# One hybrid decoder block on one Trainium2 core: the issue order of every engine drawn up on another machine model

## The chip, the core and the metric

The kernel runs on one core of a Trainium2 chip. The metric is the device time of one execution in microseconds (us); a median of several runs is given. TensorE (PE) does the matmuls, VectorE (DVE), ScalarE (ACT) and GpSimd (POOL) the elementwise work, and SyncE (SP) issues nearly all the DMA transfers. Each engine works through its own list of instructions in order; an instruction that must wait for another engine or for a transfer holds up everything behind it in its list.

## The reference, cut to what matters

Sequence 1024, width 1024, everything in float32, one layer:

```python
u = rms_norm(x, norm_mix)
u_ssm, q, k, v, f_logit, gate_logits = split(u @ w_in)
y_ssm = gelu(s5_ssm(u_ssm, ...))                     # 32 groups of 16 channels, 64 complex states
glu_a, glu_b = split(y_ssm @ w_glu);  out_a = glu_a * sigmoid(glu_b)
out_b = forgetting_attention(q, k, v, f_logit) @ w_fox_o      # 8 heads of 64, causal
...                                                  # the two branches are merged by sigmoid gates
h = x + merged @ w_mix_out
h = h + memory_cross_attention(rms_norm(h), rms_norm(mem), ...)  # 4 heads of 128, 256 memory tokens
h = h + swiglu_ffn(rms_norm(h))                      # hidden width 2816
out = rms_norm(h, norm_final)
```

## The kernel before, in words

**Arithmetic.** Every float32 operand of a matmul is split into a high part (a cast to fp32r on ACT, `split`, L178) and a low part (a subtraction on DVE or POOL, L179). A product is three matmuls: high by high, high by low, low by high (`mm3`, L168 to L170).

**Weights.** `wload` (L148 to L158) loads a block of up to 512 KB into a buffer `raw` (two buffers, DMA at L153; `stage_in` has its own at L384) and splits it into `whi` and `wlo` (four buffers each). A load can be issued only when the split of the block two loads earlier has run.

**Stages, in the order of the text.**

- `stage_in`: norms and transposes of `mem` and `x` (tiles `xt`, loaded at L351), keys and values of the memory (`w_mem_kv`), the first part of `w_in`. The small parameters of the state-space branch (`prow`, `ldr`, `craw`, `b_re`, `b_im`, `dbc`, L1132 to L1148) are loaded here too.
- `stage_ssm`: the state-space branch, with the gate logits' GEMM beside it.
- `Fox`: the attention, head by head: projections of later heads (weights loaded at L1540 and L1541), row maxima (`row_max`, L1593, and `max_row`, which sends them through the DMA `hb<-mr`, L1610), scores (L1620 to L1633), values (L1645 to L1654), and the division. During the last heads the outputs `yh`, `yl` of the state-space branch (L1698) and blocks of `wg_d` (gating weights, L153) are loaded for what follows.
- `stage_tail`: outputs of the two branches (`Glu`, `fox_part`), the mix, the memory attention (`mem_out` is its output projection), the FFN and the last norm.

**FFN.** The products go by a seven-product scheme for 2x2 blocks (`prod`, L868; the seven activation blocks are A11, A12, S4, A22, S1, S2, S3). The loop runs over 22 blocks j of the hidden width. `start(j)` does A11 and A12, `middle(j)` S2, S3 and S1, `end(j)` S4 and A22. L896 reads the bank after S4, L898 and L899 after A22, and L900 on POOL makes `g`. `w_first`, `w_sums` and `w_last` prepare the weights from `raw` and `rawb` (`w_fetch`, L805); `w_last` splits the last pair, `wdh` and `wdl`, and is the last reader of `raw`. `gated` stores sums of `g` (`c_d`), and `out_fetch` and `out_sums` prepare the second GEMM's weights (`t_d`). The second GEMM (`o_mm`, L1005) comes after the loop. PSUM has eight banks: mm 3, sc 2, pv 2, misc 1.

**What sets the order.** The text interleaves the stages by hand: an order string in `stage_in`, `weave` and `filler` lists elsewhere, and some edges "issue this after that" (`issue_after`). Within these and the data dependences, the tile framework's scheduler decides when the block `with TileContext` closes. It runs through a model of the machine and picks, for each engine, which ready instruction comes next. The semaphore waits follow from the list that results. The framework has two such models.

## Time and profile before

| what | value |
|---|---|
| median of 3 runs | 1588.8 us (1587.95 to 1590.42) |
| span of the profiled execution, first to last instruction | 1586.7 us |
| PE busy in the span | 1534.0 us, 97% |
| DVE, ACT, POOL busy | 1019.5, 655.2, 254.3 us |
| mean granted TensorE clock | 0.988 |

For the profiled execution only its span is given; the median of the other executions lies 2.1 us above it. In the profile a row reads: start, duration, engine, line, operation, destination<-sources. SPq rows are the issues of transfers, not the transfers.

### The profile page before, as it was taken

Reading aid. Unit: us, or ns where it says so; the run is one execution under the profiler, and the core shown is the slowest. Engines: PE = TensorE matmul, PEld = TensorE weight load, DVE = VectorE, ACT = ScalarE, POOL = GpSimd, SP = SyncE. Lnnn points to the kernel's source line nnn. Section 1 sums busy time; section 2 is a strip of 40 time slices with the busy share of each in tenths; the row PEclk is TensorE's granted clock in tenths of the full one; section 3 lists DMA queues with packets and bytes.
Section 4 is the critical chain, followed back from the end, with each engine's and each line's share of the span. In section 5 each row is a group of like instructions: output and inputs, shape, how many; then the busy total and the mean of one; then the engine's idle time right before and its main releaser. Section 6 shows DMA issues by size and latency. Waiting matters only on the chain.

```text
span 1586.7 us, 20446 instructions
## 1 busy us (share of the span) xinstructions
PE 1534.0 (97%) x7313; PEld 1261.3 (79%) x7313; DVE 1019.5 (64%) x1850; ACT 655.2 (41%) x1173; POOL 254.3 (16%) x335
## 2 busy tenths in 40 slices
PE   7799999999999899999999999999999999999997
PEld 6578888898777668888888778888888888788885
DVE  6666445344688687675555697766677776565555
ACT  6422434323576553222435564333333333254342
POOL 2027653200212124110002200100000000000001
PEclk8899999999999999999999999999999999999999
DMA  7764445652023736357412186555444554796642
GB/s 266 125 132 80 127 131 110 130 145 30 18 52 48 186 95 208 125 172 259 160 46 75 54 283 239 170 164 163 155 153 160 166 162 156 261 391 223 195 150 106
DMA packets 197940, 240.86 MB, mean 152 GB/s; under 512 B 35448, under 2 KB 126488, under 8 KB 197328
## 3 DMA queue, kind: packets, MB, share of 16 engines
q1 hardware_dynamic: 191216, 223.84, 48.2%
q10 hardware_dynamic: 6624, 15.73, 2.6%
q8 instruction: 57, 0.93, 0.2%
q14 instruction: 43, 0.35, 0.1%
HBM read 165.60 MB, written 75.86 MB: 152 GB/s over the span
## 4 chain that ended last, share of the span: by engine, by line
PE 75%; DVE 8%; DMA 7%; issue 4%; POOL 3%; ACT 2%; SPq 1%; DVEq 0%; POOLq 0%; ACTq 0%
PE mm L868 14%; PE mm L168 7%; PE pv L868 7%; PE mm L170 7%; PE mm L169 7%; PE mm L1005 4%; PE sc L868 3%; PE sc L1005 3%; PE pv L1005 3%; PE sc L168 3%; PE sc L169 3%; PE sc L170 3%; DMA raw<-in_w_in_dram 2%; PE misc L1005 1%; PE pv L168 1%
## 5 line engine op out<-in xcount | busy, mean ns | idle before, releaser
L179 DVE TENSOR_TENSOR wlo<-raw,whi 128x1024 fp32r<-128x1024 f32 (+2 forms) x121 | 132.0, 1094 | 135.1 <-ACT whi L178 133.9
L178 ACT CAST whi<-raw 128x1024 fp32r<-128x1024 f32 (+2 forms) x124 | 116.1, 940 | 220.0 <-DMA raw<-in_w_ffn_in_dram 54.1
L168 PE MATMUL mm<-uh,whi 128*128 128x512 f32 x344 | 138.8, 404 | 2.8 <-ACT whi L178 2.7
L170 PE MATMUL mm<-uh,wlo 128*128 128x512 f32 x344 | 136.5, 397 | 1.7 <-DVE wlo L179 1.7
L169 PE MATMUL mm<-ul,whi 128*128 128x512 f32 x344 | 136.4, 396 | 0.0
L179 DVE TENSOR_TENSOR ol<-or,oh 128x1024 fp32r<-128x1024 f32 x73 | 89.3, 1224 | 71.6 <-ACT oh L178 70.3
L178 ACT CAST oh<-or 128x1024 fp32r<-128x1024 f32 x73 | 76.8, 1052 | 105.3 <-PE mm L1005 33.6
L900 POOL TENSOR_TENSOR g<-a,c 128x512 f32<-128x512 f32 x22 | 35.2, 1600 | 392.8 <-ACT a L899 373.9
L170 PEld LDWEIGHTS mm<-uh,wlo 128*128 128x128 f32 x344 | 65.7, 191 | 16.5 <-DVE wlo L179 3.1
L1630 POOL TENSOR_TENSOR pl<-pf,ph 128x512 fp32r<-128x512 f32 (+1 forms) x32 | 39.7, 1239 | 241.1 <-DVE ph L1629 196.1
L168 PEld LDWEIGHTS mm<-uh,whi 128*128 128x128 f32 x344 | 65.9, 192 | 15.5 <-ACT whi L178 3.2
L169 PEld LDWEIGHTS mm<-ul,whi 128*128 128x128 f32 x344 | 66.0, 192 | 11.3
L197 POOL TENSOR_TENSOR r<-ms,mhalf 128x1 f32<-128x1 f32 x26 | 15.1, 582 | 354.9 <-DVE ms L193 344.5
L1627 ACT ACTIVATE pf<-sc 128x512 f32<-128x512 f32 (+1 forms) x96 | 46.5, 490 | 46.3 <-DVE sc L1623 28.6
L868 PE MATMUL pv<-S3h,we 128*128 128x512 f32 x176 | 58.1, 389 | 0.0
L1633 DVE TENSOR_TENSOR pl<-pf,ph 128x512 fp32r<-128x512 f32 (+2 forms) x64 | 35.1, 550 | 10.2 <-ACT ph L1632 9.5
L1005 PE MATMUL mm<-oh 128*128 128x512 f32 x106 | 41.2, 389 | 0.0
L1005 PE MATMUL mm<-ol,oh 128*128 128x512 f32 x106 | 41.2, 389 | 0.0
L1005 PE MATMUL mm<-oh,ol 128*128 128x512 f32 x106 | 41.2, 389 | 0.0
L168 PE MATMUL mm<-yh,whi 128*128 128x512 f32 x104 | 40.9, 393 | 0.0
L168 PE MATMUL sc<-uh,whi 128*128 128x512 f32 x104 | 40.8, 393 | 0.0
L170 PE MATMUL mm<-yh,wlo 128*128 128x512 f32 x104 | 40.6, 390 | 0.0
(580 smaller groups left out, 4537.5 us busy)
## 6 DMA issues: line engine op xcount, KB each, us to landing
or<-c_d SPq DMA_DIRECT2D x77, 256.0 KB
raw<-in_w_in_dram SPq DMA_DIRECT2D x22, 512.0 KB
wo<-in_w_ffn_out_dram SPq DMA_DIRECT2D x22, 512.0 KB
c_d<-g SPq DMA_DIRECT2D x44, 256.0 KB
t_d<-wo SPq DMA_DIRECT2D x44, 256.0 KB
or<-t_d SPq DMA_DIRECT2D x44, 256.0 KB
raw<-in_w_ffn_in_dram SPq DMA_DIRECT2D x20, 512.0 KB
rawb<-in_w_ffn_in_dram SPq DMA_DIRECT2D x20, 512.0 KB
```

The source lines that it names most:

```text
L168: T.matmul(ps, lh, rh, start=first, stop=False)
L169: T.matmul(ps, lh, rl, start=False, stop=False)
L170: T.matmul(ps, ll, rh, start=False, stop=last)
L178: self.A.copy(hi, src)
L179: (self.G if pool_lo else self.V).tensor_sub(lo, src, f32(hi))
L197: self.G.tensor_tensor(out=r, in0=v, in1=self.mhalf[:, 0:n], op=ALU.pow)
L868: T.matmul(ps, l_[:, k, :], r_, start=first and k == 0 and i == 0, stop=k == 3 and i == 2, skip_group_check=True)
L900: G.tensor_mul(g[:, 512:], a1, c1)
L1005: T.matmul(ps, l_[:, gi], r_[:, 512:], start=n < 3 and p == 0 and k == 0 or n == 7 and p == 0 and k == 0, stop=p == NP - 1 and k == 2, ski ...
L1627: self.exp = A.activation(pf[:, off:], ps[:, off:], AF.Exp)
L1630: G.tensor_sub(pl[:, off:], pf[:, off:], f32(ph[:, off:]))
L1633: V.tensor_sub(pl[:, off:], pf[:, off:], f32(ph[:, off:]))
```

## The change

The scheduler is told to run on its timeline model instead of its core model. It is one argument; no instruction of the kernel's text is changed, added or removed.

```diff
-    with _tile.TileContext(nc) as tc:
+    with _tile.TileContext(nc, schedule_with_timeline_sim=True) as tc:
         hybrid_block_kernel(tc, *args)
```

Laid side by side, the two issue orders have the same counts on every engine. On PE an instruction moves by 18 places in the mean, by up to 120 at most; on DVE by 4 in the mean, on ACT and SP by 2, on POOL by less than one. The places of the larger moves are `stage_in` (small parameters earlier in SP's list), the last heads of `Fox`, `mem_out` with the entry to the FFN, and the FFN loop. From the second FFN GEMM to the end the lists are the same.

For the FFN loop the order on PE is, each name being a product of 12 matmuls:

```text
before: A11(j) A12(j) S4(j-1) A22(j-1) S2(j) S3(j) S1(j) | A11(j+1) ...
after:  S4(j) S2(j+1)x2 A22(j) S2(j+1)x10 S3(j+2) A11(j+3)x2 A12(j+3)x2 S1(j+1) A11(j+3)x10 A12(j+3)x10 S4(j+1) ...
```

(the second line shows a part of a pattern that spans two blocks).

## The prediction

> **What bounds the kernel now.** I read the page first (busy times, slices, chain), then the table by stage, then single rows at the places where the issue order changes.
>
> ```profile
> span 1586.7 us, 20446 instructions
> PE 1534.0 (97%) x7313; PEld 1261.3 (79%) x7313; DVE 1019.5 (64%) x1850; ACT 655.2 (41%) x1173; POOL 254.3 (16%) x335
> PEclk8899999999999999999999999999999999999999
> PE 75%; DVE 8%; DMA 7%; issue 4%; POOL 3%; ACT 2%; SPq 1%; DVEq 0%; POOLq 0%; ACTq 0%
> raw<-in_w_ffn_in_dram SPq DMA_DIRECT2D x20, 512.0 KB
> ```
>
> PE is busy for 97% of the span, and three quarters of the chain that ends last is PE. The change alters no instruction, only the order in which each engine issues them. An order cannot shorten 1534.0 us of matmuls; it can only remove or add idle time of PE. What there is to remove is 1586.7 − 1534.0 = 52.7 us, and the table by stage says where (stretch, length, PE busy, PEld, DVE, ACT, POOL, granted clock, DMA share, GB/s):
>
> ```profile
> 0.00:80.00 80.00, 61.42 (x307) 50.17 (x307) 54.13 (x140) 43.40 (x74) 13.85 (x16) 0.85 0.75 194
> 80.00:500.00 420.00, 413.63 (x2198) 346.85 (x2198) 241.89 (x552) 173.59 (x300) 126.44 (x226) 1.00 0.43 94
> 500.00:580.00 80.00, 71.16 (x331) 51.14 (x331) 61.98 (x150) 47.77 (x91) 15.59 (x12) 0.98 0.54 133
> 580.00:840.00 260.00, 259.82 (x1193) 214.25 (x1192) 165.09 (x242) 85.24 (x159) 37.33 (x28) 1.00 0.48 155
> 840.00:975.00 135.00, 129.60 (x653) 104.72 (x652) 97.91 (x227) 78.39 (x220) 21.11 (x24) 0.99 0.48 170
> 975.00:1340.00 365.00, 365.00 (x1611) 301.93 (x1610) 258.93 (x367) 131.05 (x215) 31.64 (x20) 1.00 0.49 157
> 1340.00:1390.00 50.00, 47.28 (x208) 38.50 (x207) 26.69 (x33) 15.87 (x20) 3.56 (x2) 1.00 0.77 262
> 1390.00:1586.70 196.70, 186.11 (x822) 153.76 (x820) 112.92 (x143) 79.95 (x98) 4.80 (x8) 0.98 0.62 212
> ```
>
> Idle PE time by stage: head 18.6, state-space stage and first attention heads 6.4, last attention heads 8.8, branch outputs 0.2, memory attention 5.4, FFN loop 0, its exit 2.7, output GEMM and end 10.6. So a better order can win at two places, the head and the last heads, 27 us together at most. In the FFN loop, 365 us of 365, it can only lose. That asymmetry is the core of the forecast.
>
> **The change part by part.** I laid the issue orders of the two kernels side by side, engine by engine. From the output GEMM to the end they are identical: nothing changes in the last row but one term carried over, the exit. In the state-space stage matmuls move by 16 places at most, with no wait of size behind them: I take 0 for both. Four parts remain.
>
> Head. The queue of SP (it issues the loads and, being in order, blocks on the first one whose buffer isn't free):
>
> ```profile
> 8.27 0.91 SPq L351 DMA_DIRECT2D xt<-in_x_dram  x2
> 16.33 0.38 SPq L384 DMA_DIRECT2D raw<-in_w_mem_kv_dram  x1
> 38.84 0.38 SPq L384 DMA_DIRECT2D raw<-in_w_in_dram  x1
> 39.27 4.72 SPq L1141 DMA_DIRECT2D craw<-in_c_re_dram  x3
> 44.04 3.58 SPq L1141 DMA_DIRECT2D craw<-in_c_im_dram  x4
> 51.76 1.12 SPq L384 DMA_DIRECT2D raw<-in_w_in_dram  x2
> 42.64 1.05 ACT L178 CAST whi<-raw 128x1024 fp32r<-128x1024 f32 x1 [1.04 <-DMA raw<-in_w_mem_kv_dram]
> ```
>
> Before, SP issues nothing between 9.2 (8.27 + 0.91) and 16.33, where `raw` waits for its buffer; and from 39.27 to 51.76 it issues small state-space parameters, while the second w_in load stands behind them. After, ten of those parameters and three tiles of x stand ahead of the load of 16.33, the other parameters ahead of the next mem_kv loads, and none between the w_in loads. For: the 12.5 us stretch vanishes. The w_in load behind it needs the buffer whose cast ran at 42.64 to 43.69; with the low part (1.2) and the handover it could go at about 45.5, 6 us sooner, and if it lands sooner too, at most the 10 of the 18.6 idle us that lie behind it are won. Against: the ten small issues take 4.5 to 9 us (0.45 each as the x tiles at 8.27, 0.9 as the four at 44.04), the three tiles 1.4, in a gap of 7.1, and two of the tiles wait for their own buffers there. The load of 16.33 comes 0 to 6 us later, and with two `raw` buffers everything behind it too, the w_in loads included; with a colder PE say 8. Both act on one chain, so I take −2, near the middle; bounds −10 and +8.
>
> [...] The granted clock of 0.85 in the first 80 us, against 1.00 later, shows that idle PE time there is paid twice. [...]
>
> Last heads (500 to 580). The idle stretch and its queue:
>
> ```profile
> 516.00:523.00 7.00, 4.26 (x21) 2.76 (x19) 2.33 (x7) 2.09 (x4) 0.75 (x1) 1.00 0.71 177
> 506.42 8.55 SPq L153 DMA_DIRECT2D raw<-wg_d  x2
> 521.54 1.04 ACT L178 CAST whi<-raw 128x1024 fp32r<-128x1024 f32 x1 [4.85 <-DMA raw<-in_w_in_dram]
> 524.06 0.70 SPq L1610 DMA_DIRECT2D hb<-mr  x1
> 526.20 0.39 SPq L1698 DMA_DIRECT2D yh<-y_d  x1
> 545.82 0.58 SPq L1698 DMA_DIRECT2D yl<-y_d  x1
> ```
>
> The loads themselves stay where they are, so the 2.7 us that PE loses before 523 stay as well. After, another `raw<-wg_d` (its buffer comes free only after the cast of 521.54, 1.04 us and its low part) and eleven loads of y stand ahead of `hb<-mr`, the row maxima that the next head's scores need. Eleven issues of 0.39 to 0.58 are 4.3 to 6.4 us, with waits for landings up to 10: `hb<-mr` moves from 524.06 to about 530 to 535. To cover it, 20 projection matmuls and nine row-maximum units of the following head are moved ahead of those scores: 20 × 0.227 (2.72 us per 12, row below) is 4.5 us, and the nine units of about the same matmul at 0.3 each add 3 to 4. So 6 to 11 us late against 8 of cover: −2 to +3 there. The output projection of the attention moves ahead of the last head too and needs loads of att_d; the trace of before shows no such wait, and I bound it by as much idle time again as the stage has now, 8.8. The other way, 8.8 − 2.7 = 6 us of its idle time lie after 523 and could go. Bounds −6 and +12; I take +4, just above the bracket's upper end, since the moved projection can only add.
>
> Memory attention and entry to the FFN (840 to 975). The matmuls of `mem_out` go by weight block over five banks instead of product by product, the transposes of the norm come later. 5.4 us idle; half of that can go, and as much again can come: 0, bounds −5 and +5. [...]
>
> FFN loop. Before, per hidden block j, one product follows another in an even period; after, it runs one block further ahead, in a pattern of two blocks, with A11(j+3) begun only 36 matmuls after S4(j). The rows of the loop:
>
> ```profile
> 993.44 5.44 PE mm L868 x24
> 998.88 2.72 PE sc L868 x12
> 1061.48 0.69 DVE L896 SCALAR_TENSOR_TENSOR g<-mm,a 128x512 f32<-128x512 f32 x1 [0.52 <-PE mm L868]
> 1063.97 0.69 DVE L179 TENSOR_TENSOR wdl<-rawb,wdh 128x512 fp32r<-128x512 f32 x1 [1.80 <-PE pv L868]
> 1066.54 0.38 SPq L805 DMA_DIRECT2D raw<-in_w_ffn_in_dram  x1
> 1072.81 1.05 ACT L178 CAST whi<-raw 128x1024 fp32r<-128x1024 f32 x1 [5.26 <-DMA raw<-in_w_ffn_in_dram]
> 1086.69 0.38 SPq L805 DMA_DIRECT2D raw<-in_w_ffn_in_dram  x1
> 1090.67 1.05 ACT L178 CAST whi<-raw 128x1024 fp32r<-128x1024 f32 x1 [0.86 <-DMA raw<-in_w_ffn_in_dram]
> ```
>
> A matmul takes 2.72/12 = 0.227 us, so 36 are 8.2 us. In every second block the new order hangs the next weights on S4(j): L896 (0.69), behind it on DVE the two halves of `wdl` (0.69 each) which free the `raw` buffer, then SP's load, 6.27 us (1066.54 to 1072.81) or 3.98 us (1086.69 to 1090.67) to its cast, the cast of 1.05. Sum 7.1 to 9.4, with some 0.3 for handovers 7.4 to 9.7: 0.8 us to spare or 1.5 us late. Before, that load also follows the `wdl` halves, but its product stands a whole period later. With 20 loads there are ten such pairs: 0 to 15 us. I take 0.5 us each, +5; the other half of the blocks has some 16 us of slack and costs nothing. What hides the chain is those 36 matmuls; if the `wdl` halves waited also for A22(j), 14 matmuls later (3.2 us), each pair would be 2.4 to 4.7 us late.
>
> Sum: −2 + 4 + 0 + 5 = +7 against the span of 1586.7, so 1593.7. The median of the runs, 1588.8, is 2.1 above this span; I carry 2.1 over: 1595.8, rounded 1596. About 0.2%, 3.2 us, is what a measurement of this kernel can tell from no change.
>
> **The rivals.** (a) Faster: the parameters do fit into SP's idle 7 us, w_in comes 4 to 10 us sooner, the earlier y and wg_d loads take 2 to 4 of the 8.8 us idle in the last heads, and the FFN's chain takes the shorter transfer (3.98). Then −6 to −14 and no loss: about 1575 to 1583, 1579 in the middle. For it: the blocked stretch at 9.2 is plain in the rows; against: the buffers, not SP, set when `raw` may load.
>
> (b) Clearly slower: in the FFN loop the freeing of `raw` drifts behind A22. Ten pairs of 2.4 to 4.7 us are 24 to 47 us, with the +2 of the other parts 1615 to 1638. It decides where the raw load is issued later after S4(j) than 8.2 − 3.98 − 1.05 = 3.2 us, even with the shorter transfer; PE then shows a gap behind `ACT whi` in each second block. For it: the 36 matmuls leave no slack at the longer transfer; against: the order puts the `wdl` halves ahead of the wait for A22.
>
> (c) Nothing to measure: PE-bound stages stay so, the head's and the heads' shifts cancel: 1586 to 1592.
>
> (d) The interleaving itself costs: matmuls change the PSUM bank every one or two instructions in `mem_out` and in the loop, PE idles a little at each change and its clock falls. At the head's 0.85 the FFN loop's 365 us would become 429: +64, 1653. In the row 80 to 500, where attention and projection already alternate between banks, the clock is 1.00 with 413.63 of 420 busy, so I give it little. [...]
>
> **How the numbers follow.** Forecast (+2 to +17, likeliest +7): 0.43. Rival (a) 0.27. (b) 0.13. (c) 0.15. (d) 0.02. The range leaves out about 0.1 at each end: the better half of (a) below, most of (b) and (d) above: 1579 to 1618; the likeliest case alone is 1591 to 1606. Faster by over 0.2%: (a), 0.27. Within: (c), 0.15. Slower: the rest, 0.58.
>
> **What would show it.** Head: SP issues at about 10 to 16 us and no parameter after the first w_in load; PE idle in 0 to 80 about 16 to 17 us. Last heads: `hb<-mr` after the y loads, PE idle in that stage 12 to 13 us instead of 8.8. FFN loop: one gap of about 0.5 us behind `ACT whi` in each second block, in all 5 us. The loop at full density would show that step wrong and move the result to (a) or (c); gaps over 2 us would mean (b). From the output GEMM on the two traces must agree but for an offset.

## The result, and the profile after

The changed kernel took 1661.8 us in the median of four runs (1661.07 to 1661.98), the kernel before 1589.6 us on the same chip: a ratio of 1.0449, 95% interval 1.0434 to 1.0463. That is 72 us slower. The forecast was 1596, with a range up to 1618: the sign was right, the size ten times too small.

The page after (span, busy time by engine, clock by slice, shares of the chain that ended last, which could be followed back over 60% of the span only):

```profile
span 1660.2 us, 20434 instructions
PE 1566.1 (94%) x7313; PEld 1283.7 (77%) x7313; DVE 1015.4 (61%) x1850; ACT 655.3 (39%) x1173; POOL 257.7 (16%) x335
PEclk7899999999999799999999899999999999999999
PE 54%; DVE 3%; DMA 2%; ACT 1%; issue 0%; POOL 0%; SPq 0%; DVEq 0%; ACTq 0%
```

The same 7313 matmuls are busy for 1566.1 us, not 1534.0: 32.1 us more. PE is idle for 1660.2 − 1566.1 = 94.1 us, not 52.7: 41.4 us more. So two fifths of the 73.5 us between the spans is not waiting at all but matmuls that ran longer, and the reason, for most of it, stands in the clock column of the table by stage (stretch, length, PE, PEld, DVE, ACT, POOL busy, granted clock, DMA share, GB/s):

```profile
0.00:80.00 80.00, 53.76 (x268) 44.16 (x269) 45.12 (x102) 37.32 (x60) 11.99 (x15) 0.81 0.75 194
500.00:580.00 80.00, 68.29 (x274) 49.60 (x274) 51.83 (x128) 38.73 (x72) 11.77 (x9) 0.85 0.53 116
840.00:975.00 135.00, 120.23 (x585) 99.12 (x585) 65.11 (x161) 55.03 (x161) 20.84 (x22) 0.92 0.14 51
1060.00:1400.00 340.00, 339.32 (x1497) 280.65 (x1496) 235.02 (x340) 119.72 (x197) 28.59 (x18) 1.00 0.49 160
```

The clock is 0.85 and 0.92 where it was 0.98 and 0.99. The same times no longer hold the same work (500 to 580 holds 274 matmuls, 331 before), so stages cannot be compared by their times. I lined the two traces up at equal amounts of matmul work done, and read how far the changed kernel lies behind. Each trace is one execution, and single executions of the kernel before took 1587 to 1595 us, so a difference of two or three us in one stage means little:

| work, by its time in the kernel before | lag at its end | gained there | forecast |
|---|---|---|---|
| head, 0 to 140 | 14.3 | +14.3 | −2 |
| state-space stage, first heads, to 380 | 9.7 | −4.6 | 0 |
| last heads, to 700 | 41.9 | +32.2 | +4 |
| branch outputs, memory attention, FFN entry, to 1030 | 69.4 | +27.5 | 0 |
| FFN loop, to 1340 | 70.6 | +1.2 | +5 |
| its exit, to 1400 | 74.8 | +4.2 | 0 |
| output GEMM, end | 74.5 | −0.3 | 0 |

**Head.** SP's queue (issues of loads), and PE's longest wait:

```profile
12.80 4.45 SPq L1141 DMA_DIRECT2D craw<-in_c_re_dram  x4
21.17 0.40 SPq L384 DMA_DIRECT2D raw<-in_w_mem_kv_dram  x1
28.60 4.44 SPq L1148 DMA_DIRECT2D dbc<-in_d_skip_dram  x1
51.03 4.56 SPq L384 DMA_DIRECT2D raw<-in_w_in_dram  x2
...
66.61 1.22 PE L168 MATMUL mm<-uh,whi 128*128 128x512 f32 x2 [8.32 <-ACT uh L178]
```

The parameters do fill SP's idle time, but the third load of `w_mem_kv` goes at 21.17 instead of 16.33 and the first of `w_in` at 51.03 instead of 38.84.

**Last heads.** The loads of y stand ahead of the row maxima, as forecast, and PE's issue order has long runs of one kind (issues of SP; then the first and last row of one run on PE):

```profile
558.11 0.36 SPq L1698 DMA_DIRECT2D yh<-y_d  x1
...
566.38 0.98 SPq L1610 DMA_DIRECT2D hb<-mr  x1
```

```profile
446.58 0.44 PE L168 MATMUL mm<-uh,whi 128*128 128x512 f32 x1
...
450.74 0.39 PE L168 MATMUL mm<-uh,whi 128*128 128x512 f32 x1
```

From the first of these two rows to the second, 4.4 us, stand 19 projection matmuls and nothing else. In the whole issue list of the last heads the kernel before mostly has groups of three to six projection matmuls with three to eight other steps between them; the changed kernel has run after run of 17 to 21, and between them stretches of 13 to 42 steps with none or a few. The other steps are scores, values and row maxima, which depend on work of ACT or DVE. The four largest of PE's waits between 390 and 600 (us in total, times, longest), in the changed kernel:

```profile
PE mm L168 <- ACT whi L178: 4.4, 2, 4.2
PE mm L1593 <- DVE mc L1598: 3.5, 5, 1.7
PE mm L1593 <- ACT hb L1568: 2.6, 5, 1.1
PE pv L1645 <- DVE ph L1629: 2.6, 5, 1.4
```

Only the first is behind a load; the others are many short waits behind DVE and ACT. The clock during and behind the first of these waits, in steps of 2 us (every second one is shown):

```profile
550.00:552.00 2.00, 0.00 (x0) 0.00 (x0) 0.00 (x0) 0.00 (x0) 0.00 (x0) 0.80 0.99 254
554.00:556.00 2.00, 1.15 (x4) 0.44 (x3) 2.00 (x5) 1.99 (x4) 0.00 (x0) 0.50 0.15 47
558.00:560.00 2.00, 2.00 (x6) 1.53 (x5) 1.85 (x4) 1.73 (x3) 0.00 (x0) 0.50 0.39 115
562.00:564.00 2.00, 2.00 (x10) 1.58 (x10) 0.30 (x2) 0.00 (x0) 0.00 (x0) 1.00 1.03 293
```

Within the wait of 4.2 us, which ends at 553.4, the clock goes to 0.50 and stays there for some 10 us, also where PE is busy all the time: six matmuls in 2 us at 558, ten at 562. In the work of 380 to 700 PE's idle time grows by 15 us, its busy time by 17, with 34 us at half clock (sums over the clock record) where the kernel before has 3.4; from 700 to 1030 by 17 and 10.

### The profile page after: what moved, and what is told of

Same layout as the page of the kernel before. It is cut to its first block, busy times and chain, and to the rows that moved or that the text cites. A ratio compares the mean times of both kernels' runs of the same rounds, so it can differ in the third digit from the quotient of the medians.

```text
span 1660.2 us, 20434 instructions
## 1 busy us (share of the span) xinstructions
PE 1566.1 (94%) x7313; PEld 1283.7 (77%) x7313; DVE 1015.4 (61%) x1850; ACT 655.3 (39%) x1173; POOL 257.7 (16%) x335
## 4 chain that ended last, share of the span: by engine, by line
PE 54%; DVE 3%; DMA 2%; ACT 1%; issue 0%; POOL 0%; SPq 0%; DVEq 0%; ACTq 0%
PE mm L868 14%; PE pv L868 7%; PE mm L1005 4%; PE sc L868 4%; PE sc L1005 3%; PE mm L168 3%; PE mm L169 3%; PE mm L170 3%; PE pv L1005 3%; PE misc L1005 2%; PE sc L168 2%; PE sc L170 1%; PE sc L169 1%; PE pv L169 1%; PE pv L170 1%; PE pv L168 1%
## 5 line engine op out<-in xcount | busy, mean ns | idle before, releaser
L179 DVE TENSOR_TENSOR wlo<-raw,whi 128x1024 fp32r<-128x1024 f32 (+2 forms) x121 | 131.9, 1093 | 120.7 <-ACT whi L178 119.3
L168 PE MATMUL mm<-uh,whi 128*128 128x512 f32 x344 | 140.2, 410 | 13.8 <-ACT uh L178 8.8
L179 DVE TENSOR_TENSOR ol<-or,oh 128x1024 fp32r<-128x1024 f32 x73 | 88.9, 1223 | 69.0 <-ACT oh L178 68.5
L168 PEld LDWEIGHTS mm<-uh,whi 128*128 128x128 f32 x344 | 67.5, 197 | 29.3 <-ACT uh L178 9.4
L197 POOL TENSOR_TENSOR r<-ms,mhalf 128x1 f32<-128x1 f32 x26 | 18.6, 718 | 365.2 <-DVE ms L193 337.1
L178 ACT CAST we<-rawb 128x512 fp32r<-128x512 f32 x20 | 12.5, 623 | 80.4 <-PE pv L868 49.5
L1595 DVE CUSTOM_DVE_ANT_0 junk<-mm,tri 128x128 bf16<-128x128 f32 (+1 forms) x64 | 31.1, 485 | 19.9 <-PE mm L1593 18.3
L868 PEld LDWEIGHTS pv<-S3h,we 128*128 128x128 f32 x176 | 34.2, 195 | 10.2 <-ACT S3h L178 3.0
L168 PE MATMUL sc<-uh,whi 128*128 128x512 f32 x104 | 40.8, 392 | 0.0
```

The source lines that it names most:

```text
L168: T.matmul(ps, lh, rh, start=first, stop=False)
L178: self.A.copy(hi, src)
L179: (self.G if pool_lo else self.V).tensor_sub(lo, src, f32(hi))
L197: self.G.tensor_tensor(out=r, in0=v, in1=self.mhalf[:, 0:n], op=ALU.pow)
L868: T.matmul(ps, l_[:, k, :], r_, start=first and k == 0 and i == 0, stop=k == 3 and i == 2, skip_group_check=True)
L1595: B.V.tensor_tensor_reduce(out=B.junk[:, :n], in0=ps[:, :n], in1=self.tri[:, 512 - n:512], scale=1.0, scalar=-3.0e38, op0=ALU.add, op1=ALU ...
```

## The experiments

Each of the first ten keeps the text and pins issue orders: the instructions of an engine are chained in a given order with edges that cost nothing at run time (e8_mid_after, pinned on every engine, runs no slower than the kernel before). Where only some lists are pinned, the scheduler draws up the others with the pinned ones in view, so they are neither exactly those of the kernel before nor those of the changed one.

```diff
         hybrid_block_kernel(tc, *args)
+        _pin(tc, nc)      # for each engine in ORDER: add_manual_dep(next, last, NoSync, "issue order")
```

**Which stage: e1_head, e2_heads, e3_mem, e4_loop.** The order of the kernel before on every engine, but in one stretch the changed kernel's: to 130 us, 382 to 700, 700 to 1030, from 1030 on.

> Every engine's list is pinned, instruction by instruction: the changed kernel's order up to about 130 us of the kernel before (norms, memory keys and values, first projection, state-space parameters), the order before from there on. Theory L (each stage pays for its own order): in the traces the changed kernel is 14 us behind at 130 us, so this run is 11 to 16 us slower than before, about 1603. Rival K (the loss is a chain: one late stage makes the next one collide with its transfers): the later stages lose in part too because the head is late, so this run alone is 20 us slower or more.

> The changed order only for what the kernel before does from about 382 to 700 us (last attention heads, branch outputs), the order before elsewhere. Theory L: in the traces the distance between the kernels grows from 10 to 42 us there, so this run is 27 to 35 us slower than before, about 1620. Rival K: with the head on time most of it goes, under 15 us slower.

> The changed order only for what the kernel before does from about 700 to 1030 us (mix output, memory attention, norm and entry of the FFN), the order before elsewhere. Theory L: the distance grows from 42 to 70 us there, so this run is 24 to 32 us slower than before, about 1617. Rival K: under 12 us slower.

> The order before up to about 1030 us, the changed order from there to the end (FFN loop with its two-block pattern, the exit into the output GEMM). Theory L: 0 in the loop and 4 at the exit, so 2 to 6 us slower than before, about 1593. Rival (my forecast for the loop): 0.5 us in each second block, 5 us in the loop, with small idle gaps of PE there. Rival K: no difference within 1 us.

| kernel | median, us | before | ratio, 95% interval |
|---|---|---|---|
| e1_head | 1606.6 | 1592.0 | 1.0095 (1.0072 to 1.0118) |
| e2_heads | 1624.2 | 1592.0 | 1.0202 (1.0168 to 1.0236) |
| e3_mem | 1619.5 | 1592.0 | 1.0179 (1.0150 to 1.0207) |
| e4_loop | 1595.5 | 1592.0 | 1.0030 (1.0014 to 1.0045) |

The four losses are 14.5, 32.2, 27.5 and 3.5 us, each with an interval of 2.5 to 5.5 us to either side, 78 in all; less the 4.6 that the state-space stage gains, 73. All four lie in the ranges of theory L and outside those of rival K: each stage pays for itself, and none hands on a lag that these times could show. In e4_loop the loop itself is full (first fence, table by stage), and the 3.5 us come at the exit, as one wait of the second GEMM for its first activations (second fence, waits of PE from 1330 to 1410), which the changed kernel has too, at 3.9:

```profile
1000.00:1340.00 340.00, 340.00 (x1501) 281.53 (x1501) 232.81 (x339) 119.94 (x196) 26.87 (x17) 1.00 0.48 155
```

```profile
PE sc L1005 <- ACT oh L178: 4.0, 1, 4.0
```

**Which engine's list: e5_pe_before, e6_sp_before, e7_pe_after.** The timeline model decides everything but PE (e5) or but SP (e6), pinned as before; and the core model decides everything but PE, pinned as after (e7).

> The timeline model decides all lists but PE's, which is pinned over the whole kernel to the order of the kernel before. In the head (to 130 us) SP's list then is almost that of the changed kernel. Theory P (in the last heads and in the memory attention PE's order is the cause: matmuls that wait for nothing stand in bunches instead of between the steps that wait for ACT and DVE; in the head SP's order is the cause): the two later losses go, the head's 14 us stay: 10 to 18 us slower than before, about 1606. Rival S (SP's list is the cause in all stages): stays 50 us slower or more, about 1645.

> The timeline model decides all lists but SP's, which is pinned over the whole kernel to the order of the kernel before; PE's list stays near that of the changed kernel. Theory P: only the head's loss goes: 50 to 64 us slower than before, about 1647. Rival S: under 15 us slower, about 1600.

> The core model as before decides all lists but PE's, which is pinned over the whole kernel to that of the changed kernel; SP's list in the head stays that of the kernel before. Theory P: the later losses appear and the head's doesn't, or only in part, since PE's list in the head waits for what the parameters bring: 48 to 65 us slower than before, about 1646. Rival S: under 15 us slower.

Measured: e5 1624.5 (1.0204, 1.0183 to 1.0225), e6 1663.9 (1.0467, 1.0438 to 1.0496), e7 1667.5 (1.0475, 1.0449 to 1.0501), each against 1591.3. Pinning PE's new order alone brings the whole loss (e7: 10.0 us in the head, 26.5 between 380 and 620, 32 in the memory stage, 6 at the exit), and that although SP's loads in e7's head go at 16.70 and 38.88 as before. The lists of DVE and ACT there are drawn up around PE's: DVE's lies 3.3 places in the mean from that of the kernel before and 1.7 from the changed kernel's, so the loss isn't PE's list set against the old lists of the others. The late weight loads are not needed for the head's loss; e6 says the same, where SP's old order left 10.4 us of lag in the head. Both runs are slower than theory P expected, which put the head's loss on SP. But without PE's new order 33 us remained too (e5), twice what I expected.

**The parts alone: e9_sp_timeline, e10_pe_sp_before.** The timeline model decides SP's list alone (e9), or those of DVE, ACT and POOL alone (e10); the rest is pinned as before.

> The timeline model decides SP's list alone; PE, DVE, ACT and POOL are pinned over the whole kernel to the order of the kernel before. In the head SP's list then is that of the changed kernel, with the parameters ahead of the memory weights. Theory A (the lists add up: SP's list costs the head's 10 us, as the run with PE pinned showed at 100 us, and little later): 8 to 14 us slower than before. Rival B (SP's list does no harm when the other lists are those of before): within 3 us of before.

> The timeline model decides DVE's, ACT's and POOL's lists; PE's and SP's are pinned over the whole kernel to the order of the kernel before. Theory A: what the run with PE pinned still lost behind the head (17 us in the last heads, where PE waited for DVE's row maxima, and 12 in the memory attention) is due to DVE's and ACT's lists, so 20 to 30 us of it stay: about 1615. Rival B (it was SP's list): under 8 us slower.

Measured: e9 1598.9 (1.0059, 1.0038 to 1.0080), e10 1624.7 (1.0212, 1.0187 to 1.0237), each against 1590.6. SP's list costs 8.4 us, nearly all of it in the head, as theory A had it. The lists of DVE, ACT and POOL cost 34, above theory A's 20 to 30, of which 12.5 in the head, 18 in the last heads, 7 in the memory stage. With e7's 76 that is 119 against 72 for all together, so the losses do not add up. Nor need they: DVE's list in e10 is nearer to that of the kernel before (1.6 places in the mean) than to the changed kernel's (3.3), so e10 shows what the timeline model's lists can lose beside PE's old one, and not a part of the 72. The head loses 8 to 12.5 us in e5, e7, e9 and e10 alike, whichever lists are new; what its loss hangs on stays open.

**The gain alone: e8_mid_after.** The changed kernel's order only between 150 and 382 us.

> Every list pinned: the changed order only for what the kernel before does from about 150 to 382 us (state-space stage and first attention heads), the order before elsewhere. There the distance between the two traces shrinks from 14.3 to 9.7 us, so theory L (each stage pays for its own order) expects 3 to 5 us faster than before, about 1585: a kernel better than both. Rival: the gain there is only the catching up of a kernel that was late, and this run is within 1 us of before.

Measured 1589.8 against 1591.3, 0.9987 (0.9975 to 0.9999). The 4.6 us are gained by 380, but 5.5 are lost again by 460 in the profiled run. So the result, 1.5 us faster, lies between theory and rival, and it is not a version worth having. In the changed kernel too the lag grows by 4.9 us between 380 and 400, so part of its 32.2 may be the 4.6 handed back.

**What a gap costs: e11_gaps.** The order of before, and on POOL, in every second block of the FFN loop, 7 to 14 copies of `wlo` onto itself, which hold up one product's weights.

```diff
-        B.split(*a_, ra)
+        B.split(*a_, ra); _hold(j, B.G, a_[1])    # j = 4, 6 .. 18: G.tensor_copy(lo, lo) 7, 8 .. 14 times
```

> The kernel before with its order pinned, and in every second block of the FFN loop (j = 4, 6, ... 18) 7 to 14 copies in place on POOL of the low part of the weights of A11(j), so that PE, dense there, has to wait for a moment that grows from block to block. It measures the price of an idle gap of PE by itself. Theory C (a gap costs its length, and from a certain length on a stretch of half the clock on top, 3.4 us or more, that is 1.7 us or more of lost work): the kernel gets slower by the sum of the gaps plus at least 1.7 us for each of the longer ones; the clock's record shows one stretch of 0.5 behind each of those. Rival D (only the gap itself counts): the clock stays at 1.00 in the loop, and the time grows by the sum of the gaps.

Measured 1642.4 against 1590.6, 1.0327 (1.0305 to 1.0350). The gaps did not grow with the number of copies as planned; all eight are alike. The wait of PE behind them, then four of the 2 us steps around one of them:

```profile
PE mm L868 <- ACT a L885: 34.3, 8, 4.8
```

```profile
1106.00:1108.00 2.00, 0.05 (x1) 0.00 (x0) 1.92 (x4) 1.14 (x2) 0.00 (x0) 1.00 0.16 60
1110.00:1112.00 2.00, 2.00 (x5) 1.62 (x6) 2.00 (x2) 0.97 (x2) 1.14 (x1) 0.50 0.68 202
1112.00:1114.00 2.00, 2.00 (x7) 1.52 (x6) 0.28 (x1) 0.11 (x1) 0.00 (x0) 0.50 1.07 325
1118.00:1120.00 2.00, 2.00 (x10) 1.65 (x10) 1.93 (x4) 1.11 (x2) 0.00 (x0) 1.00 0.07 29
```

Eight gaps of 4.3 us in the mean cost 53.0 us of lag, 6.6 each: the gap and 2.3 us more, in a stretch at half clock behind it. That is theory C's outcome; its 3.4 us are the shortest stretch at half clock in the traces of the kernel before and of the changed one. In this loop a gap of 4.3 us was paid one and a half times.

**Bunching made on purpose: e12_bunch.** The kernel before with one tuple of its text changed, scheduled by the core model: the projection steps of the heads stand in two clumps of eight, not spread.

```diff
-PSLOT = (0, 0, 1, 2, 3, 3, 4, 5, 5, 6, 7, 8, 9, 10, 10, 11)
+PSLOT = (2,) * 8 + (7,) * 8
```

> The kernel before (core model, nothing pinned) with one line of its text changed: the sixteen parts of each head's projection, of three matmuls each, no longer spread over the twelve steps of the attention but eight at step 2 and eight at step 7; PE's list then has 24 projection matmuls in a row, twice per head, and the score, value and row-maximum matmuls without any between them. In the changed kernel they stand 17 to 21 in a row. Theory P (bunches of matmuls that wait for nothing starve the steps between them): PE waits for ACT's exponentials, DVE's splits and row maxima, some 3 to 5 us for each of the five or six heads concerned, and the clock drops on top: 12 to 30 us slower than before. Rival Q (the bunches do no harm; what costs is where the row maxima and their bank releases stand): within 4 us of before.

Measured 1625.6 against 1592.2, 1.0212 (1.0171 to 1.0252): 33 us, a little more than theory P's 12 to 30 and far from rival Q. That it is as much as e2_heads is chance: the bunches here are longer than the changed kernel's (24 with 30 to 43 other steps between them), and the loss lies elsewhere, 32.8 us in the work of 400 to 500, where the changed kernel loses 14.3. The lag grows by 6.6 to 10.1 us in each 20 us of work between 420 and 500. Of the 32.8 us, 15.4 are idle time and 17.4 matmuls that ran longer. PE's waits between 380 and 580, first in e12_bunch, then the same two in the kernel before, which has no wait for L1595 there at all:

```profile
PE sc L1620 <- ACT pf L1627: 7.4, 8, 2.1
PE mm L1593 <- DVE mc L1595: 7.2, 8, 1.4
```

```profile
PE sc L1620 <- ACT pf L1627: 2.5, 3, 1.5
```

Eight scores wait for ACT's exponential and eight row-maximum matmuls for DVE's row maxima, and the projections that used to fill these waits have gone by in a block. None of the waits is longer than 2.1 us, yet the clock falls (2 us steps of e12_bunch):

```profile
492.00:494.00 2.00, 0.61 (x4) 0.25 (x2) 0.74 (x3) 1.96 (x4) 0.00 (x0) 1.00 0.03 2
494.00:496.00 2.00, 1.88 (x10) 1.69 (x11) 1.39 (x5) 1.83 (x5) 0.00 (x0) 0.96 0.03 8
496.00:498.00 2.00, 2.00 (x6) 1.54 (x6) 1.42 (x7) 0.14 (x1) 0.73 (x1) 0.50 0.00 0
```

**Breadth and bunching in the memory attention: e13_breadth, e14_bunch_mem.** The kernel before with `mem_out` by weight block over four banks instead of product by product; and with the memory attention's two weaves replaced by one part after the other, so that the wait-free `mem_q` and `mem_out` come ahead of the scores, turns and values.

```diff
-        for c in range(2):
-            ps = B.bank()
-            for h in range(MH):
-                B.mm3(ps, ...)
+        for h in range(MH):
+            for q in range(4):              # 2 row tiles x 2 halves, a bank each
+                B.mm3(ps_[t, q], ...)
```

```diff
-    weave([lambda h=h: mem_q(h, 1) for h in range(MH)], cross(0))
+    in_turn([lambda h=h: mem_q(h, 1) for h in range(MH)], cross(0))      # main, then side
...
-    weave([lambda t=t: mem_out(t) for t in range(4)], cross(1) + ...)
+    in_turn([lambda t=t: mem_out(t) for t in range(4)], cross(1) + ...)
```

> The kernel before (core model, nothing pinned) with the text of mem_out changed: for two row tiles at a time the four products go by weight block, four banks side by side, and all four end together, instead of one product after the other. The changed kernel does this with up to five banks. Theory V (it is this order of the products that costs in the memory attention: their sums, the norm and the transposes behind them begin later and then stand alone): 8 to 25 us slower than before. Rival W (it is the placing of the wait-free matmuls against the steps of the cross attention and the transposes, of which the order of the products is no part): within 4 us of before.

> The kernel before (core model, nothing pinned) with two lines of its text changed: mem_q of the second half is done before the steps of the first half's cross attention, and mem_out of the first half before those of the second, instead of woven between them. The wait-free matmuls then stand in bunches and the scores, turns and values of the cross attention follow each other with little between. Theory W (in the memory attention too it is the bunching that costs): PE waits at the turns and values for the softmax on DVE, ACT and POOL, with the clock dropping on top: 8 to 30 us slower than before. Rival X (the steps hide each other, as eight of them are open at a time): within 4 us of before; then the memory attention's loss stays unexplained.

Measured: e13 1595.4 against 1591.5, 1.0019 (1.0006 to 1.0031); e14 1620.8 against 1591.5, 1.0183 (1.0164 to 1.0203). The order by weight block costs 4 us (1 to 5 by the interval), as rival W had it; bunching costs 29, as theory W had it, of which 26 lie in the memory attention. PE's waits there in e14_bunch_mem, 840 to 1010, and from the waits of the changed kernel (840 to 1030) and of the kernel before (800 to 980) the row that answers to the first:

```profile
PE misc L693 <- DVE ptl L179: 9.4, 5, 2.2
PE misc L223 <- DVE xs L217: 6.5, 2, 5.6
PE mm L168 <- ACT pe L680: 3.8, 2, 2.5
```

```profile
PE misc L693 <- DVE ptl L179: 3.8, 2, 1.9
```

```profile
PE misc L693 <- DVE ptl L179: 1.1, 1, 1.1
```

The turn (L693) waits for the split of what PE turned just before, for 9.4 us where the kernel before lost 1.1. In the changed kernel the same wait, 3.8, is the largest of this stage. But e14 bunches far more than the changed kernel does: 96 and 66 wait-free matmuls in a row against 39 and 30 at most, and up to 80 matmuls of the cross attention without any between them against 26. And a first 7.7 of the changed kernel's 27.5 us fall in the work of 800 to 840, where PE waits 4.5 us for tiles of the norm (L223 and L168) and where e14 loses nothing. So e14 shows that bunching can cost this much, and not that it does in the changed kernel.

**Bunching undone in the changed kernel: e15_spread, e16_spread_core.** The changed kernel's PE list, but in the last heads the runs of 17 to 21 projections are dealt out in threes and sixes over the steps behind them. The other lists by the timeline model (e15) or the core model (e16, to be set against e7).

> The changed kernel with one thing undone. Its whole PE list is kept but for the last heads: there the runs of 17 to 21 projection matmuls are broken up and dealt out in threes and sixes over the steps that follow them (none is issued earlier than in the changed kernel). All other lists are left to the timeline model. Theory P (the bunching of projections that wait for nothing is what costs in the last heads): the 27 to 32 us of that stage shrink to 5 to 15, a time of 1637 to 1650 against 1662. Rival R (the lateness of hb<-mr behind the loads of y and att_d, or the order on DVE and ACT, costs there): the stage keeps 20 us or more, 1655 to 1670.

> The same PE list with the projections dealt out, the other lists left to the core model. To be compared with the kernel that had the changed kernel's PE list as it is and the core model for the rest (1667.5, of it 26.5 us in the last heads). Theory P: the stage falls by 15 to 22 us, 1645 to 1653. Rival R: within 6 us of 1667.

Measured: e15 1651.1 against 1592.2, 1.0376 (1.0359 to 1.0393); e16 1660.4, 1.0429 (1.0398 to 1.0460). Between 380 and 620 the lag grows by 15.6 us instead of 27.3 (e15 against after) and by 18.5 instead of 26.5 (e16 against e7). In the plain attention, work of 400 to 500, it grows by 5.0 instead of 14.3 (e16 against e7: 5.3 instead of 15.0). The table row of this work in the kernel before, in the changed kernel and in e15_spread:

```profile
400.00:500.00 100.00, 99.35 (x485) 75.56 (x483) 77.61 (x197) 64.58 (x124) 19.43 (x16) 1.00 0.22 41
```

```profile
414.40:528.70 114.30, 106.81 (x484) 78.47 (x483) 78.44 (x198) 64.10 (x125) 21.18 (x16) 0.97 0.19 36
```

```profile
413.70:518.80 105.10, 99.34 (x489) 76.96 (x488) 77.66 (x204) 66.30 (x127) 21.25 (x16) 1.00 0.20 39
```

Of the 9.2 us that come back, 7.5 are busy time, which is back at its value before with the clock at 1.00, and only 1.7 are waits; in e16 against e7 it is 4.3 and 5.5. From 500 to 560 the lag still grows by 9.5, after 12.0. There the loads are as they were: the wait for a weight block stays (4.0 us), and the row maxima still go behind the loads of y. PE's wait between 385 and 600, and SP's issue, in e15_spread:

```profile
PE mm L168 <- ACT whi L178: 4.0, 1, 4.0
```

```profile
570.36 0.68 SPq L1610 DMA_DIRECT2D hb<-mr  x1
```

So the bunching is a true cause in the changed kernel, worth 8 to 12 us of the 27; in both pairs the lists of DVE, ACT and POOL are all but the same (DVE's moves by 0.2 places in the mean). By the medians e15 is 10.7 us faster than the changed kernel, clear of noise, and e16 7.2 us faster than e7, with intervals that overlap. For e15 the 15.6 us lie just outside theory P's 5 to 15 and farther from the rival's 20 or more, for e16 the 8 us given back lie between P's 15 to 22 and the rival's 6 at most. Each theory holds a part. What the rest is made of is not separated: the late loads, the new order among scores, values and row maxima, and the lists of DVE and ACT are candidates.

## Why the prediction was right or wrong

- **"An order can only remove or add idle time of PE."** Wrong, and the widest error: 32 of the 73.5 us are the same matmuls, run longer, mostly at a lower clock. I had read this from the head's 0.85 ("paid twice") and then priced it nowhere else. Over the whole kernel 41.4 us of added idle time cost 73.5, 1.8 us for each; in the head 11 cost 14, in the last heads (380 to 700) 15 cost 32, in the memory stage 17 cost 28. For single gaps of 4.3 us in dense work the price was one and a half (e11_gaps).
- **Last heads, +4 (−6 to +12), measured +32.** The predicted tell was there: `hb<-mr` at 566.38 behind y loads from 558.11, and PE idle for 80 − 68.29 = 11.7 us in 500 to 580, where I had said 12 to 13. But that idle time was read in a window of time that now holds 57 matmuls fewer. The step that failed is the cover: I counted the 20 projections that stand together ahead of the scores as 4.5 us of cover for one late load, and did not ask which other waits they had been covering, one every few steps. (The cover was also summed too high: nine units at 0.3 are 2.7, not 3 to 4.) Making longer bunches costs 33 us (e12_bunch), and undoing them in the changed kernel gives 8 to 12 of its 27 back, partly as a higher clock, partly as shorter waits. The lists of DVE, ACT and POOL, which I did not cost at all, lost 18 us in these heads when the timeline model drew them up beside PE's old list (e10). The step stays open for the other 15 to 19 us.
- **Memory attention, 0 (−5 to +5), measured +27.5.** I bounded it by its idle time before, as if idle time could at most double. That bound failed: the idle time in this stage grew by 17 us, and its matmuls ran 10 us longer. Bunching `mem_q` and `mem_out` alone can cost 29 us (e14_bunch_mem), but with far longer bunches. For the changed kernel itself the cause stays open; the bunching there was not undone, and 7.7 us are lost in work where e14 loses nothing.
- **Head, −2 (−10 to +8), measured +14.** Both bounds were built on SP's queue. That the parameters push the weight loads was right (21.17 for 16.33, 51.03 for 38.84), and SP's list alone costs 8.4 us (e9). No run shows the 2 us that "a colder PE" adds in the upper bound (8 instead of 6); measured in 0 to 80, the granted clock is 0.81 instead of 0.85, and PE is idle for 26.2 us instead of 18.6. But with the loads in place PE's new list costs 10.0 (e7), and new lists of DVE, ACT and POOL cost 12.5 (e10). What failed is that only SP's list was priced, as though the other engines could follow any order of theirs.
- **FFN loop, +5 (0 to 15), measured +1.** The step with the most working was the least needed. The predicted half-us gap in each second block shows once in ten pairs; 339.32 of 340 us are busy, and the missing 0.68 are this wait (load, cast, the first product that needs it, in the changed kernel):

```profile
1123.58 0.38 SPq L805 DMA_DIRECT2D raw<-in_w_ffn_in_dram  x1
1127.71 1.05 ACT L178 CAST whi<-raw 128x1024 fp32r<-128x1024 f32 x1 [2.56 <-DMA raw<-in_w_ffn_in_dram]
1128.81 0.50 PE L868 MATMUL mm<-A11h,whi 128*128 128x512 f32 x1 [0.68 <-ACT whi L178]
```

In the other nine the cast ends 0.2 to 1.3 us before its product. So the chain was right at its short end (0.8 to spare): the term that was too large is the load, 3.7 to 4.9 us from issue to cast, and not 6.27. Rival (b) falls with it, though by a narrow margin.

- **Exit, 0, measured +4.** One wait of 3.9 us for the second GEMM's first activations, not foreseen. **State-space stage, 0, measured −4.6.** **Output GEMM on:** identical but for the offset, as forecast.
- **Rival (d)** had the right symptom at a chance of 0.02: a lower clock where the order changes. Its cause was wrong. From 936 to 943 the changed kernel's `mem_out` goes from bank to bank every one or two matmuls, and PE is busy all the time at full clock:

```profile
936.00:943.00 7.00, 7.00 (x34) 5.87 (x33) 2.26 (x6) 1.23 (x3) 0.00 (x0) 1.00 0.01 2
```

The loop, with its products interleaved, runs at 1.00 too, and changing banks every third matmul costs 1 to 5 us in `mem_out` (e13_breadth). A lower clock does stand behind the long waits (the 4.2 us before 553.4, then 0.50). It stands behind short ones too: in e12_bunch the clock is 0.50 from 496 on, the wait at 494.12 is 1.51 us long, and none from 380 to 580 is longer than 2.1 us.

- **The chances.** "Slower" had 0.58 and came. That the sign came out right is partly luck: most of the forecast's +7 was the loop's +5, which lost 1. The range ended at 1618 since the last heads and the memory attention were given no way to lose more than about their idle time again; these two lost most.

## What to carry to other kernels

When two issue orders are compared, look not at how far instructions move but at how the wait-free ones are spread: wherever steps that depend on other engines now stand back to back, expect waits between them. The FFN loop bore its new order for about 1 us, with less than 1.5 us to spare in each second block; the stages of short chains between engines did not, and their idle time before was no bound on what they could lose. In this kernel a single gap of 4.3 us cost one and a half times its length (e11_gaps: 6.6 us), and many short waits about twice their sum (e12_bunch: 15.4 idle us cost 32.8). Compare stages at equal work, not at equal times.

## What the runs showed of the hardware that was not expected

**The clock was at half speed behind short waits as well**, as the rows of e12_bunch above show (0.50 from 496 to 498, no wait from 380 to 580 over 2.1 us); in the changed kernel it is at half speed for 117.7 us in all, 40.1 before (sums over the clock record; 8.5 and 9.4 of them behind the last matmul). Up to the last matmul the half-speed stretches of both are 3.4, 6.8, 10.2 or 13.7 us long, so the least that a fall of the clock cost here was 3.4 us at half speed.

**DVE was slower while POOL copied.** The gaps in e11_gaps came by another way than planned. Rows of POOL and DVE around one of them:

```profile
1092.76 12.92 POOL L1819 CAST wlo<-wlo 128x1024 fp32r<-128x1024 f32 x9 [7.74 <-DVE wlo L179]
1093.12 0.68 DVE L890 SCALAR_TENSOR_TENSOR c<-c,pv 128x512 f32<-128x512 f32 x1
1096.02 1.52 DVE L921 SCALAR_TENSOR_TENSOR s<-g 128x512 f32<-128x512 f32 x1
1103.25 0.68 DVE L877 TENSOR_TENSOR a<-a,sc 128x512 f32<-128x512 f32 x1
```

While POOL copied (nine copies in 12.92 us, 1.44 each), DVE's operations on two SBUF tensors took up to 1.52 us, near one copy each and 2.2 times as long as otherwise (L921 takes 0.685 in the mean in the kernel before; L179 on a `wlo` of 128x512 takes 1.52 at 1101.80 and 0.69 at 1106.90, behind the copies); those that read one operand from PSUM (L890, L877) kept their 0.68. DVE's queue fell behind, with it ACT's L885, for which PE waited (3.94 us at 1109.99).
